# Where SyncE looks at the semaphores of the last eight loads: in front of the last store or behind it

## The chip, the cores and the metric

The kernel runs on one core of a Trainium2 chip. The metric is the device time of one execution in microseconds (us); medians are over runs. The span in a profile goes from the first to the last recorded instruction.

## The reference

It computes the skewness of each of 1024 rows of 8192 float32 numbers:

```python
mean = np.mean(x, axis=-1, keepdims=True)
std = np.std(x, axis=-1, keepdims=True)
z = (x - mean) / (std + 1e-8)
return np.mean(z ** 3, axis=-1).astype(np.float32)
```

## The kernel before

The rows are taken as eight blocks of 128. Each block arrives in two to seven loads, all issued by SyncE into a pool of eight buffers. ScalarE squares and sums, VectorE multiplies and sums the cubes, TensorE sums the columns. A short closing stage makes `skew`, and SyncE stores it (4 KB). The parts that matter here:

```python
for b, widths in enumerate(UNITS):
    ...
    for k, w in enumerate(widths):
        xt = xpool.tile([P, w], FP, tag="x", name=f"x_{b}_{k}")
        nc.sync.dma_start(out=xt, in_=xv[b, :, c0 : c0 + w])
        ...
# ... closing arithmetic of the last two blocks
nc.gpsimd.tensor_tensor(out=rr, in0=var2, in1=expo[:, 0 : NB - F], op=ALU.pow)
nc.vector.tensor_reduce(out=num, ...)
nc.vector.tensor_tensor(out=skew[:, F:NB], in0=num, in1=rr, op=ALU.mult)
nc.sync.dma_start(out=ov, in_=skew)
```

Nothing in this text waits for a semaphore: the framework adds the waits. In the trace of this kernel each DMA that SyncE issues signals on one of eight semaphores, called lanes here, in rotation. At the end of the program the framework makes SyncE check that everything is finished, then all five engines meet (from 89.04 us, when SyncE joins, to the end of the span at 89.729). In the built program, SyncE's end is this (each line an instruction with its waits; `lane3` is the store's):

```
semaphore instruction   lane3 (old value)
store                   VectorE's skew
--- last block of the program
semaphore instruction   lane3 (the store), lane2
semaphore instruction   lane4, lane1
semaphore instruction   lane5, lane0
semaphore instruction   lane6, VectorE
semaphore instruction   lane7, TensorE
drain                   ScalarE
drain                   joins the meeting of the five engines
```

Of the kernel before, what the change touches and what calls it, by code (L numbers as in the profile page):

```python
# [8 lines left out]
FP = mybir.dt.float32  # L9
AF = mybir.ActivationFunctionType  # L10
ALU = mybir.AluOpType
X_AXIS = mybir.AxisListType.X


# [17 lines left out]
def _slices(w):  # L32
    n = -(-w // SUB_MAX)
    step = -(-w // n // 128) * 128
    return [(s, min(s + step, w)) for s in range(0, w, step)]
# [3 lines left out]
def kernel(  # L39
# [5 lines left out]
    nc = tc.nc  # L45
# [13 lines left out]
    xv = x.rearrange("(p b) c -> b p c", b=NB)  # L59
# [11 lines left out]
    def small(name, n):  # L71
        return onep.tile([P, n], FP, tag=name, name=name)
# [22 lines left out]
    def close_first_blocks():  # L95

        m2, m3 = small("m2a", F), small("m3a", F)
        for dst, src in ((m2, s2u), (m3, s3u)):
            nc.vector.tensor_reduce(  # L99
                out=dst, in_=src[:, 0 : F * K].rearrange("p (b c) -> p b c", c=K),  # L100
                axis=X_AXIS, op=ALU.add,
            )
        m1sq, m1sq3, nm1 = small("m1sqa", F), small("m1sq3a", F), small("nm1a", F)
        nc.scalar.copy(out=m1a[:, nw:F], in_=s1ps[:, nw:F])
        nc.scalar.activation(out=m1sq, in_=m1a, func=AF.Square)
        nc.scalar.activation(out=m1sq3, in_=m1a, func=AF.Square, scale=third)
        nc.scalar.activation(out=nm1, in_=m1a, func=AF.Copy, scale=-3.0)
        g = nc.gpsimd
        var, rr = small("vara", F), small("rra", F)
        g.tensor_tensor(out=var, in0=m2, in1=m1sq, op=ALU.subtract)  # L110
        g.tensor_tensor(out=m1sq3, in0=m1sq3, in1=var, op=ALU.add)  # L111
        g.tensor_tensor(out=m1sq3, in0=m1sq3, in1=nm1, op=ALU.mult)  # L112
        g.tensor_tensor(out=m3, in0=m3, in1=m1sq3, op=ALU.add)  # L113
        g.tensor_tensor(out=rr, in0=var, in1=expo, op=ALU.pow)  # L114
        g.tensor_tensor(out=skew[:, 0:F], in0=m3, in1=rr, op=ALU.mult)  # L115

    def close_on_act(b):

        m2, m1sq, nm1, v3 = (small(f"{t}_{b}", 1) for t in ("m2", "m1sq", "nm1", "v3"))
        p1 = s1ps[:, b : b + 1]  # L120
        var = var2[:, b - F : b - F + 1]
        act = nc.scalar.activation
        yield act(out=junk, in_=s2u[:, b * K : b * K + K], func=AF.Copy, accum_out=m2)
        yield act(out=m1sq, in_=p1, func=AF.Square)  # L124
        yield act(out=var, in_=m1sq, func=AF.Identity, scale=-1.0, bias=m2)  # L125
        yield act(out=nm1, in_=p1, func=AF.Copy, scale=-3.0)  # L126
        yield act(out=v3, in_=m1sq, func=AF.Identity, scale=1.0 / 3.0, bias=var)  # L127
        yield act(  # L128
            out=s3u[:, b * K + K - 1 : b * K + K], in_=v3, func=AF.Identity, scale=nm1
        )  # L130

    pending = iter(())
    for b, widths in enumerate(UNITS):
        tp = psum.tile([P, P], FP, tag="tp", name=f"tp_{b}")
        c0 = 0
        j = b * K
        for k, w in enumerate(widths):
            last_unit = b == L and k == len(widths) - 1
            xt = xpool.tile([P, w], FP, tag="x", name=f"x_{b}_{k}")
            nc.sync.dma_start(out=xt, in_=xv[b, :, c0 : c0 + w])  # L140
            c0 += w
            for s, e in _slices(w):
                if last_unit:
                    sq = psum1.tile([P, e - s], FP, tag="sqps", name=f"sqps_{s}")
                else:
                    sq = sqpool.tile([P, e - s], FP, tag="sq", name=f"sq_{b}_{k}_{s}")
                nc.scalar.activation(  # L147
                    out=sq, in_=xt[:, s:e], func=AF.Square, scale=s_scale,
                    accum_out=s2u[:, j : j + 1],
                )  # L150
                cube = sqpool.tile([P, e - s], FP, tag="sq", name="cube") if last_unit else sq
                nc.vector.scalar_tensor_tensor(  # L152
                    out=cube, in0=sq, scalar=1.0, in1=xt[:, s:e],
                    op0=ALU.mult, op1=ALU.mult, accum_out=s3u[:, j : j + 1],
                )
                j += 1
            w_act = S1_ACT.get((b, k), 0)
            if w_act:
                nc.scalar.activation(  # L159
                    out=same[:, 0:w_act], in_=xt[:, w - w_act : w], func=AF.Copy,  # L160
                    scale=inv_n, accum_out=s1a[:, b : b + 1],
                )
            n = (w - w_act) // P
            for c in range(n):
                nc.tensor.matmul(  # L165
                    out=tp, lhsT=xt[:, c * P : (c + 1) * P], rhs=ident,
                    start=(k == 0 and c == 0), stop=(c0 == C and c == n - 1),
                    is_transpose=True,
                )
            if k > 0:  # L170
                next(pending, None)
                next(pending, None)
        tsb = Tsb[b % 2]
        nc.scalar.copy(out=tsb, in_=tp)  # L174
        nc.tensor.matmul(out=s1ps[:, b : b + 1], lhsT=tsb, rhs=onesn, start=True, stop=True)  # L175
        if b == F - 2:
            nc.vector.tensor_tensor(
                out=m1a[:, 0:nw], in0=s1ps[:, 0:nw], in1=s1a, op=ALU.add
            )
        if b == F - 1:  # L180
            close_first_blocks()
        if b >= F:
            pending = close_on_act(b)
    for _ in pending:
# [4 lines left out]
    nc.vector.tensor_reduce(  # L189
        out=num, in_=s3u[:, F * K :].rearrange("p (b c) -> p b c", c=K), axis=X_AXIS, op=ALU.add  # L190
    )
    nc.vector.tensor_tensor(out=skew[:, F:NB], in0=num, in1=rr, op=ALU.mult)  # L192
    nc.sync.dma_start(out=ov, in_=skew)


# [28 lines left out]
```

## Time and profile before

| | us |
|---|---|
| median of three runs (range) | 91.64 (91.61 to 91.72) |
| span of the profiled run, which took 91.50 | 89.73 |
| last load landed | 83.56 |
| `skew` finished on VectorE | 87.20 |
| store started; landed | 87.23; 88.65 |
| SyncE's first drain of the closing line; joins the meeting | 88.98; 89.04 |

The starts to the nanosecond, here and below, are read from the trace's records, since the page rounds to 0.1 us. A semaphore instruction is not counted as work, so the chain of work ends at `skew`; what comes after it has to be read from the instructions of the program's closing line (L219 here).

How to read the views: SPq, DVEq and so on are the engines' instruction queues (SP is SyncE, DVE VectorE, ACT ScalarE, POOL GpSimd, PE TensorE). EVENT_SEMAPHORE is a semaphore instruction; to look at a semaphore is to execute one that waits for it. DRAIN is an instruction of the closing line; SyncE's first one comes after its last look. "Landed" is the time of the last semaphore event recorded for a transfer (the store of the kernel before has 16 of them, from 88.473 to 88.648 us). Views are cut to the lines that are read.

### The profile page before, as it was taken

The numbers are of one execution on the slowest core, as the hardware profiler recorded it, in microseconds if no ns is written. First come the engines' busy times: TensorE is split into PE (matmuls) and PEld (weight loads), VectorE is DVE, ScalarE is ACT, GpSimd is POOL, SyncE is SP. The second block draws the span as 40 slices with busy tenths as digits, with TensorE's granted clock in tenths as the row PEclk, the third lists the DMA queues.
The fourth block names the chain that finished last, engine by engine and source line by source line (L and its number), as shares of the span: only waits on it lengthen the run. The fifth ranks groups of instructions, "written<-read, shape, count | busy, mean of one in ns | idle before, by whom it ended". The sixth has DMA issues, their size and how long they took to land.

```text
span 89.7 us, 1368 instructions
## 1 busy us (share of the span) xinstructions
PE 64.9 (72%) x504; PEld 59.3 (66%) x504; DVE 72.7 (81%) x80; ACT 72.1 (80%) x106; POOL 11.3 (13%) x14
## 2 busy tenths in 40 slices
PE   0003999892882919989998988888987798969710
PEld 0003999791872909979897977877876787848500
DVE  1000498989999298995999999999999999999970
ACT  6003999699991999859898989978979898999950
POOL 3000000000000000000000000000005999900030
PEclk9999999999999997599999999999999999999998
DMA  3999999999999999999999999999999999994000
GB/s 117 351 424 438 424 431 431 431 431 424 446 416 431 424 438 424 424 438 427 415 409 418 419 427 419 421 415 419 409 414 417 404 413 411 421 412 161 0 0 2
DMA packets 4038, 33.64 MB, mean 375 GB/s; under 512 B 576, under 2 KB 576, under 8 KB 2240
## 3 DMA queue, kind: packets, MB, share of 16 engines
q1 hardware_dynamic: 4032, 33.56, 89.7%
q8 instruction: 4, 0.07, 0.3%
q14 instruction: 2, 0.02, 0.0%
HBM read 33.55 MB, written 0.00 MB: 374 GB/s over the span
## 4 chain that ended last, share of the span: by engine, by line
DMA 73%; ACT 13%; issue 5%; DVE 4%; SPq 1%; PE 1%; DVEq 0%; ACTq 0%
DMA x<-in_x_dram 73%; ACT sq L147 9%; DVE sq L152 3%; ACT sqps L147 1%; ACT same L159 1%; SPq L140 1%; PE s1ps L175 1%; ACT tsb L174 0%; ACT s3u L128 0%; ACT v L127 0%; ACT var L125 0%; DVE num L189 0%; ACT m1sq L124 0%; DVE skew L192 0%; ACT nm L126 0%
## 5 line engine op out<-in xcount | busy, mean ns | idle before, releaser
L152 DVE SCALAR_TENSOR_TENSOR sq<-sq,x 128x2048 f32<-128x2048 f32 (+9 forms) x35 | 70.7, 2071 | 13.4 <-ACT sq L147 13.3
L165 PE MATMUL tp<-ident,x 128*128 128x128 f32 x488 | 62.6, 288 | 17.3 <-DMA x<-in_x_dram 17.2
L165 PEld LDWEIGHTS tp<-ident,x 128*128 128x128 f32 x488 | 57.9, 150 | 20.9 <-DMA x<-in_x_dram 12.7
L147 ACT ACTIVATE sq<-x 128x2048 f32<-128x2048 f32 (+9 forms) x35 | 60.6, 1734 | 10.7 <-DMA x<-in_x_dram 9.9
L110 POOL TENSOR_TENSOR vara<-m2a,m1sqa 128x6 f32<-128x6 f32 x1 | 1.8, 1822 | 67.1 <-DVE m3a L99 67.1
L147 ACT ACTIVATION_READ_ACCUMULATOR sq<-x 128x1 f32 x35 | 6.5, 186 | 0.0
L175 PEld LDWEIGHTS s1ps<-onesn,tsb 128*128 128x128 f32 x16 | 2.4, 188 | 5.2 <-ACT tsb L174 5.2
L175 PE MATMUL s1ps<-onesn,tsb 128*128 128x1 f32 x16 | 3.1, 260 | 3.3 <-ACT tsb L174 3.3
L174 ACT COPY tsb<-tp 128x128 f32<-128x128 f32 x8 | 2.0, 256 | 2.0 <-PE tp L165 2.0
L114 POOL TENSOR_TENSOR rra<-vara,expo 128x6 f32<-128x6 f32 x1 | 3.3, 3267 | 0.0
L159 ACT ACTIVATE same<-x 128x1024 f32<-128x1024 f32 x3 | 3.1, 1041 | 0.0
L152 DVE DVE_READ_ACCUMULATOR sq<-sq,x 128x1 f32 x35 | 2.9, 83 | 0.0
L111 POOL TENSOR_TENSOR m1sq3a<-m1sq3a,vara 128x6 f32<-128x6 f32 x1 | 1.9, 1868 | 0.1
L77 ACT ACT_TABLE_LOAD x1 | 1.3, 1283 | 0.7 <-PEq L208 0.7
L187 POOL TENSOR_TENSOR rr<-var,expo 128x2 f32<-128x2 f32 x1 | 0.7, 702 | 7.7 <-ACT var L125 7.7
L152 DVE SCALAR_TENSOR_TENSOR cube<-sqps,x 128x1152 f32<-128x1152 f32 x1 | 1.4, 1350 | 0.0
L113 POOL TENSOR_TENSOR m3a<-m3a,m1sq3a 128x6 f32<-128x6 f32 x1 | 1.2, 1201 | 0.1
L147 ACT ACTIVATE sqps<-x 128x1152 f32<-128x1152 f32 x1 | 1.1, 1136 | 0.1
L115 POOL TENSOR_TENSOR skew<-m3a,rra 128x6 f32<-128x6 f32 x1 | 1.1, 1069 | 0.1
L124 ACT ACTIVATE m1sq<-s1ps 128x1 f32<-128x1 f32 x2 | 0.3, 171 | 0.5 <-PE s1ps L175 0.5
L75 DVE MEMSET onesn<- 128x1 f32 x1 | 0.1, 59 | 0.8 <-PEq L208 0.8
L112 POOL TENSOR_TENSOR m1sq3a<-m1sq3a,nm1a 128x6 f32<-128x6 f32 x1 | 0.7, 697 | 0.0
(28 smaller groups left out, 6.8 us busy)
## 6 DMA issues: line engine op xcount, KB each, us to landing
x<-in_x_dram SPq DMA_DIRECT2D x8, 2048.0 KB, 23.4
x<-in_x_dram SPq DMA_DIRECT2D x4, 1152.0 KB, 27.9
x<-in_x_dram SPq DMA_DIRECT2D x4, 576.0 KB, 8.6
x<-in_x_dram SPq DMA_DIRECT2D x1, 1792.0 KB, 33.0
x<-in_x_dram SPq DMA_DIRECT2D x2, 832.0 KB, 13.9
x<-in_x_dram SPq DMA_DIRECT2D x1, 1024.0 KB, 21.1
x<-in_x_dram SPq DMA_DIRECT2D x2, 512.0 KB, 10.0
x<-in_x_dram SPq DMA_DIRECT2D x1, 960.0 KB, 13.2
```

What stands on the lines that cost most here:

```text
L77: nc.scalar.activation(out=tiny, in_=onesn, func=AF.Square)
L110: g.tensor_tensor(out=var, in0=m2, in1=m1sq, op=ALU.subtract)
L111: g.tensor_tensor(out=m1sq3, in0=m1sq3, in1=var, op=ALU.add)
L113: g.tensor_tensor(out=m3, in0=m3, in1=m1sq3, op=ALU.add)
L114: g.tensor_tensor(out=rr, in0=var, in1=expo, op=ALU.pow)
L115: g.tensor_tensor(out=skew[:, 0:F], in0=m3, in1=rr, op=ALU.mult)
L147: nc.scalar.activation(out=sq, in_=xt[:, s:e], func=AF.Square, scale=s_scale, accum_out=s2u[:, j : j + 1],)
L152: nc.vector.scalar_tensor_tensor(out=cube, in0=sq, scalar=1.0, in1=xt[:, s:e], op0=ALU.mult, op1=ALU.mult, accum_out=s3u[:, j : j + 1],)
L159: nc.scalar.activation(out=same[:, 0:w_act], in_=xt[:, w - w_act : w], func=AF.Copy, scale=inv_n, accum_out=s1a[:, b : b + 1],)
L165: nc.tensor.matmul(out=tp, lhsT=xt[:, c * P : (c + 1) * P], rhs=ident, start=(k == 0 and c == 0), stop=(c0 == C and c == n - 1), is_transp ...
L174: nc.scalar.copy(out=tsb, in_=tp)
L175: nc.tensor.matmul(out=s1ps[:, b : b + 1], lhsT=tsb, rhs=onesn, start=True, stop=True)
```

## The change

Its intent is to let SyncE see, while it would be idle anyway, that the eight last loads have landed, in front of the store, so that the closing check has less left to see once the store has landed.

```diff
+SYNC_DEP = mybir.DependencyInfo(
+    mybir.DependencyClass.Sync, mybir.DependencyReason.DATA
+)
...
+    loads = []
...
-            nc.sync.dma_start(out=xt, in_=xv[b, :, c0 : c0 + w])
+            loads.append(nc.sync.dma_start(out=xt, in_=xv[b, :, c0 : c0 + w]))
...
+    seen = nc.sync.nop()
+    for ld in loads[-8:]:
+        tc.add_manual_dep(seen.ins, ld.ins.name, SYNC_DEP)
     nc.sync.dma_start(out=ov, in_=skew)
```

`seen` is an instruction of SyncE that does nothing; each `SYNC_DEP` makes it wait for one load's semaphore.

## The prediction

> **What bounds the kernel now.** I read the page's chain of work that ended last first, then the last 4 us in order of time, then SyncE's own waits, then the instructions of the program's last line, because the change touches nothing but SyncE at the very end. The chain (section 4 of the page):
>
> ```profile
> DMA 73%; ACT 13%; issue 5%; DVE 4%; SPq 1%; PE 1%; DVEq 0%; ACTq 0%
> ```
>
> The input stream carries 73% of the 89.7 us span: the kernel is bound by 33.55 MB of loads. The change does not alter a load, a buffer or an engine's order, so those first 83.6 us should stay as they are. The chain in order of time, from the last load on:
>
> ```profile
> 76.06 7.50 DMA x<-in_x_dram
> 83.56 0.02 issue
> 83.58 1.26 ACT sqps L147 x2
> ...
> 86.76 0.18 DVE num L189
> 86.95 0.03 issue
> 86.97 0.02 DVEq L192
> 86.99 0.04 issue
> 87.04 0.16 DVE skew L192
> ```
>
> Columns are start, length and what. The last load has landed at 76.06 + 7.50 = 83.56 us; from there 3.64 us of closing arithmetic end at 87.20 with VectorE's skew. The chain stops there, as it follows only working instructions; 89.7 - 87.2 = 2.5 us of the span come after it. SyncE's own waits say what it does around there:
>
> ```profile
> SPq L193 <- DVE skew L192: 10.8, 1, 10.8
> SPq L219 <- DMA out_dram<-skew: 1.1, 1, 1.1
> ```
>
> SyncE is idle for 10.8 us in front of the store, waiting for skew, and after it waits 1.1 us for the store to land. The store and its landing:
>
> ```profile
> L193 SPq DMA_DIRECT2D out_dram<-skew x1: 348/348/348, 87.2 to 87.2; - x1
> ...
> DMA to landing us min/median/max: 1.4/1.4/1.4
> ```
>
> In the last-4-us view the store starts at 87.23, so it has landed at about 88.65. What is left, about 1.08 us, is the program's closing line, L219. Its instructions up to 89.03 us and, in a second view, from 89.03 on:
>
> ```profile
> L219 SPq EVENT_SEMAPHORE  x5: 28/28/28, 88.7 to 88.9; - x5
> ...
> L219 SPq DRAIN  x1: 7/7/7, 89.0 to 89.0; - x1
> ```
>
> ```profile
> L219 POOLq EVENT_SEMAPHORE  x4: 17/17/17, 89.1 to 89.6; - x4
> L219 SPq DRAIN  x2: 7/7/7, 89.0 to 89.3; - x2
> ```
>
> SyncE executes five semaphore instructions one after another, then a drain, then the drain by which it joins the meeting of all five engines. The rounding hides the spacing, so I took it from the trace's records. The store's last landing event is at 88.648; the five semaphore instructions start at 88.665, 88.729, 88.791, 88.855 and 88.917, the drain at 88.982, the joining drain at 89.040, and the meeting ends the span at 89.729. The pitch is (88.982 - 88.665) / 5 = 63.4 ns although each is only 28 ns long by its row. The other engines' first drains start at 85.2 (TensorE), 86.1 (GpSimd), 86.4 (ScalarE) and 87.1 (VectorE): all are waiting for SyncE, which therefore sets the end.
>
> [...] 28 ns reported, 63 ns apart, so pitch and not duration is the cost. [...] The trace has a 0.35 us issue and a 4 KB store that takes 1.42 us from its start to landing[...]; nothing in the change shortens it.
>
> **The change part by part.** The added no-operation vanishes in the build: the order of instructions lists no new one, and its eight waits are shown on the store beside the wait for skew. In the built program an instruction holds at most two waits in front of the one that carries work, so the waits become semaphore instructions:
>
> - In front of the store: before, one semaphore instruction (the store's own lane, an old value) and the store's wait for skew. After, five (one with one wait, four with two) and the same wait. Four more.
> - Behind the store: before, five holding ten waits: the eight load and store lanes, VectorE and TensorE. After, two: first one for VectorE alone, then one for the store's lane with TensorE. The seven lanes without the store need no second look, as SyncE has seen them. Three fewer, and SyncE has one more instruction in all (66 against 65).
>
> Cost in front of the store: the added four take 4 x 63 = 0.25 us. The slowest of them waits for the last load, which lands at 83.56; with one more behind it SyncE stands at the store by about 83.75. Skew is ready at 87.20. So 3.45 us of slack hide it: cost on the path 0.
>
> Gain behind the store: the first remaining instruction waits for VectorE only, which is already done, so it executes in the 1.1 us while the store flies. After the landing there is one semaphore instruction instead of five. The drain starts at 88.665 + 0.063 = 88.728 instead of 88.982: 4 x 63.4 = 0.254 us saved. Everything from the drain on, 89.729 - 88.982 = 0.747 us, should shift unchanged.
>
> Sum: span 89.73 - 0.25 = 89.48 us. The median of the time is 91.64, of which 1.9 us lie outside the span and stay. 91.64 - 0.25 = 91.39 us, a gain of 0.28%.
>
> **Rivals.**
>
> 1. *The semaphores in front delay the store.* Four at 63 ns would cost 0.25 us if they ran after skew, cancelling the gain: 91.64. For it: they do stand in front of the store in SyncE's order. Against it: all eight of their conditions are met at 83.56, 3.6 us before skew[...].
> 2. *The tail's looks are hidden already, or another engine becomes the last.* If the meeting waited for something besides SyncE, the saving would be cut; 91.5 to 91.64. Against it: the next latest drain (VectorE's) starts at 87.1 and is 174 ns long, 1.7 us before SyncE joins at 89.04, far more than 0.25.
> 3. *Only part is saved.* The VectorE look may not be finished when the store lands, if SyncE is slow to cross from the store to the last block (the store's issue ends at 87.58, the first look is ready no later than 88.665). One 63 ns instruction would return: 91.45.
> 4. *The stream shifts.* [...] the stream, which sets 73%, could move by more than the gain. The three times before span 0.11 us (91.61 to 91.72), so I allow about twice that, either way.
>
> **Range and chances.** The mechanism gives 91.39; rivals 3 and 4 lie mostly above it. I put the range at 91.18 to 91.60: the saving of 0.25 with 0.2 us of scatter either way. Two per cent would be 1.83 us in either direction; the whole stretch from skew to the end is 2.5 us, of which 1.42 is the store's own flight, so no removal of semaphore looks can reach it, and a loss of that size would take a stall of which the trace shows no sign. Faster by over 2%: 0.01. Within 2%: 0.98. Slower: 0.01.
>
> **What would show each step right or wrong.** In the changed kernel's profile the closing line should have two SyncE semaphore instructions before its first drain, the first starting before the store lands and the second within some 20 ns of the landing; the drain some 65 ns after that one and the end 0.75 us after the drain. From skew's end to the span's end should be 2.28 us instead of 2.53. The semaphore instructions on the store's line should be five, the last at about 83.7 us, and the store should still start some 30 ns after skew. The prediction is wrong if the store starts later than that after skew, if the landing takes clearly other than 1.42 us, if the first look in the last block comes after the landing, or if the span up to skew moves by more than 0.2 us.

The 0.254 us is four times the 63.4 ns read from the trace.

## The result

The changed kernel took 91.38 us in the median (91.33 to 91.61, six runs) beside 91.62 of the kernel before (91.52 to 91.72, six runs). Ratios, this kernel's time over that of before, are formed from runs taken in the same rounds, so they are not quite the ratio of the medians, nor of the means of all runs: here 0.9978, with a 95% interval of 0.9965 to 0.9991. The gain of 0.24 us between the medians is 0.26%: the same within 2%.

The profiled run of the changed kernel was its slowest, 91.61 us with a span of 89.78, so its span is no shorter than that of before. The views therefore have to be read stretch by stretch. Its chain in order of time (start, length, what):

```profile
76.52 7.35 DMA x<-in_x_dram
83.87 0.02 issue
83.89 1.26 ACT sqps L151 x2
...
87.34 0.16 DVE skew L196
```

The last load landed at 83.87 us, 0.30 later than in the profile of before. From there to the end of `skew` it is 3.64 us in both. So the stream was late in this execution and the closing arithmetic was the same. SyncE's own waits (what waited for what: total, times, longest):

```profile
SPq L198 <- DMA x<-in_x_dram: 6.9, 3, 4.5
SPq L201 <- DVE skew L196: 3.6, 1, 3.6
SPq L227 <- DMA out_dram<-skew: 1.0, 1, 1.0
```

The idle time in front of the store, one wait of 10.8 us before, is now split: 6.9 us on loads and then still 3.6 us on `skew`. The looks come before that 3.6 us, which is slack left over. The looks themselves and the store, in two views of lines L198 and L201 (count, shortest/median/longest in ns, first and last start):

```profile
L198 SPq EVENT_SEMAPHORE  x4: 17/28/2771, 76.9 to 81.1; - x4
```

```profile
L201 SPq EVENT_SEMAPHORE  x1: 28/28/28, 83.9 to 83.9; - x1
L201 SPq DMA_DIRECT2D out_dram<-skew x1: 348/348/348, 87.5 to 87.5; - x1
```

All five semaphore instructions in front of the store start by 83.92 us, and the store starts 28 ns after `skew`, as before (29 ns). The closing line, from 87 us to its first drain:

```profile
L227 SPq EVENT_SEMAPHORE  x2: 17/22/28, 87.9 to 89.0; - x2
...
L227 SPq DRAIN  x1: 7/7/7, 89.0 to 89.0; - x1
```

Two are left instead of five. The first, at 87.93, ran while the store was in flight; only the second, at 88.97, comes after the landing at 88.951. From landing to drain it is 0.084 us, where the kernel before took 0.334. From the end of `skew` to the end of the span it is 2.274 us against 2.530: 0.256 us less.

### The profile page after: what moved, and what is told of

Same layout as the page of the kernel before. It is cut to its first block, busy times and chain, and to the rows that moved or that the text cites. A ratio compares the mean times of both kernels' runs of the same rounds, so it can differ in the third digit from the quotient of the medians.

```text
span 89.8 us, 1369 instructions
## 1 busy us (share of the span) xinstructions
PE 63.8 (71%) x504; PEld 58.0 (65%) x504; DVE 72.7 (81%) x80; ACT 72.0 (80%) x106; POOL 11.3 (13%) x14
## 4 chain that ended last, share of the span: by engine, by line
DMA 57%; DVE 21%; PE 6%; ACT 5%; issue 4%; SPq 3%; DVEq 0%
DMA x<-in_x_dram 57%; DVE sq L156 20%; PE tp L169 6%; SPq L144 3%; ACT sq L151 2%; ACT sqps L151 1%; PE s1ps L179 0%; ACT v L130 0%; ACT s3u L131 0%; ACT tsb L178 0%; ACT var L128 0%; DVE num L193 0%; ACT m1sq L127 0%; DVE skew L196 0%; ACT nm L129 0%
## 5 line engine op out<-in xcount | busy, mean ns | idle before, releaser
L169 PE MATMUL tp<-ident,x 128*128 128x128 f32 x488 | 61.4, 284 | 18.6 <-DMA x<-in_x_dram 18.4
L169 PEld LDWEIGHTS tp<-ident,x 128*128 128x128 f32 x488 | 56.4, 147 | 22.5 <-DMA x<-in_x_dram 14.0
```

What stands on the lines that cost most here:

```text
L169: nc.tensor.matmul(out=tp, lhsT=xt[:, c * P : (c + 1) * P], rhs=ident, start=(k == 0 and c == 0), stop=(c0 == C and c == n - 1), is_transp ...
```

## The experiments

Theory: each semaphore instruction that SyncE executes after the store has landed costs about 63 ns; one executed while SyncE would wait anyway costs nothing. Rivals: the gain on the clock is only scatter; or the looks have to be in front of the store. Each diff is against the changed kernel; `...` marks what is left out, and the comments are added here. `AFTER_IT` is a dependency that sets the order without a wait. All kernels gave correct results. e0_after, e1_behind, e3_half and e4_full ran on one chip with nine runs of the kernel before (median 91.57 us); e2_late, b0_before, e5_after and e6_full on another with nine others (median 91.57).

### The changed kernel again (e0_after, e5_after)

No edit.

> The changed kernel once more, beside the others on one chip. Theory (each semaphore instruction that SyncE executes after the store has landed costs one pitch of 63 ns; those executed earlier cost nothing): 0.25 us under the kernel before, one semaphore instruction between landing and drain, landing to end 0.78 us. Rival (the 0.24 us seen is scatter of the load stream): a ratio to before of 0.999 to 1.001 this time.

> The changed kernel a third time, for the mean. Theory: ratio to before about 0.997, skew's end to the span's end 2.28 us. Rival (no gain on the clock): ratio 0.999 or more as in the second set of runs.

The first of these sets gave 91.53 us (91.31 to 91.60) and a ratio of 0.9990 (0.9976 to 1.0003), an interval that holds both "no gain" and most of the gain; the second gave 91.33 us (91.27 to 91.40) and 0.9971 (0.9957 to 0.9985). On the clock alone, the first set would have supported the rival. The profiles do not: from `skew`'s end to the span's end both have 2.28 us, and from landing to drain 0.084. The "landing to end 0.78" that I had written is an error of addition. It should be the 1.08 us of before less 0.25, 0.83, and 0.829 was measured. The same slip of about 0.05 us is in the expectations of e1_behind (0.78) and e4_full (0.72).

### The look behind the store (e1_behind)

```diff
...
+    st = nc.sync.dma_start(out=ov, in_=skew)
     seen = nc.sync.nop()
+    tc.add_manual_dep(seen.ins, st.ins.name, AFTER_IT)   # order only, no wait
     for ld in loads[-8:]:
         tc.add_manual_dep(seen.ins, ld.ins.name, SYNC_DEP)
-    nc.sync.dma_start(out=ov, in_=skew)
```

> The same look at the eight loads stands behind the store instead of in front of it. Theory (only being ahead of the landing matters, not being ahead of the store): SyncE executes five waits of the eight lanes in the about 1.1 us of the store's flight, 5 x 63 = 0.32 us, so they are done before the landing; the time equals the changed kernel's within 0.05 us, 0.25 us under before; landing to end 0.78 us. Rival (the looks have to be in front of the store): the time is that of the kernel before, landing to end 1.08 us.

It took 91.45 us (91.30 to 91.48), ratio 0.9979 (0.9967 to 0.9992). The four looks (L202) and then the closing line's SyncE instructions up to 89 us:

```profile
L202 SPq EVENT_SEMAPHORE  x4: 17/28/28, 87.8 to 88.0; - x4
```

```profile
L231 SPq EVENT_SEMAPHORE  x2: 17/22/28, 88.3 to 88.9; - x2
L231 SPq COMPARE_BRANCH  x1: 33/33/33, 88.1 to 88.1; - x1
L231 SPq DRAIN  x1: 7/7/7, 89.0 to 89.0; - x1
```

The looks ran from 87.85 on, behind the store's issue, and were finished by 88.3. The branch to the closing line (COMPARE_BRANCH) carries the wait for one lane, and the first semaphore instruction behind it is the look for VectorE. The store landed at 88.871. From landing to drain it is 0.082 us, from `skew` to the end 2.276, the changed kernel's numbers. So being in front of the store is not what mattered in this kernel. Being ahead of its landing was.

### Half of the loads (e3_half)

```diff
-    for ld in loads[-8:]:
+    for ld in loads[-4:]:
```

> The look covers the last four loads only. In the built program three semaphore instructions stand in front of the last drain instead of five (before) or two of which one is early (changed). The first of the three waits for the store's lane, so all three come after the landing. Theory: 2 x 63 = 0.13 us saved against before, half of the whole change; landing to end 0.95 us. Rival (the gain comes from one particular wait or from scatter): the whole 0.25 us or nothing.

The ratio was 0.9997 (0.9985 to 1.0010), at 91.60 us (91.40 to 91.70), with the median above that of before: the clock shows nothing of the 0.13 us. For the profiled run, the slowest of the five at 91.70, the profile gives a reason: its last load landed at 83.859, late in the range found below. For the other four no landing is on record, so the missing gain is not explained for them. The tail is where the theory puts it, between the two kernels:

```profile
L227 SPq EVENT_SEMAPHORE  x3: 28/28/1047, 87.9 to 89.1; - x3
L227 SPq DRAIN  x1: 7/7/7, 89.1 to 89.1; - x1
```

Three semaphore instructions stand before the drain, and from landing to drain it is 0.191 us, against 0.084 with one and 0.334 with five. The longest is recorded with 1047 ns. I had expected it to wait for the store first. In the built program its first condition is a load, met at once, so it had started at 87.92 and was waiting for its second, the store. That made it 18 ns cheaper than two more pitches (0.084 + 2 x 0.063 = 0.209).

### No semaphore instruction behind the landing (e4_full, e6_full)

```diff
...
+    st = nc.sync.dma_start(out=ov, in_=skew)
     seen = nc.sync.nop()
-    for ld in loads[-8:]:
-        tc.add_manual_dep(seen.ins, ld.ins.name, SYNC_DEP)
-    nc.sync.dma_start(out=ov, in_=skew)
+    tc.add_manual_dep(seen.ins, st.ins.name, AFTER_IT)
+    for i in loads[-8:] + [mm, la, pw, last]:   # last of PE, ACT, POOL, DVE
+        tc.add_manual_dep(seen.ins, i.ins.name, SYNC_DEP)
```

> The look stands behind the store and covers the eight loads and the last instructions of TensorE, ScalarE, GpSimd and VectorE, so that the drain itself waits for the store's lane and no semaphore instruction is left between landing and drain. Theory: one more pitch of 63 ns saved than the changed kernel, 5 x 63 = 0.32 us under before; landing to end 0.72 us. Rival (the first instruction after a landing has a floor, or SyncE is not done with six waits before the landing): no better than the changed kernel.

> The kernel with no semaphore instruction between landing and drain once more, for the mean. Theory: skew's end to the span's end 2.21 us, 0.32 us under before, ratio to before about 0.9965. Rival: no better than the changed kernel of the same set.

The two sets gave 91.40 us (91.20 to 91.44), ratio 0.9973 (0.9960 to 0.9985), and 91.26 us (91.19 to 91.33), ratio 0.9965 (0.9952 to 0.9977). Here is the closing line of the first of them, SyncE alone, up to the first drain:

```profile
L231 SPq COMPARE_BRANCH  x1: 33/33/33, 88.1 to 88.1; - x1
L231 SPq DRAIN  x1: 7/7/7, 88.8 to 88.8; - x1
```

No semaphore instruction is left; the drain waits for the store itself and starts 17 ns after its landing, in both profiles. From `skew` to the end it is 2.207 and 2.209 us, 0.07 less than the changed kernel and 0.32 less than before. Against the kernel before, both intervals exclude 1. Against the changed kernel its median is lower in both sets (91.40 against 91.53, 91.26 against 91.33), but the single runs overlap, so that step rests on the profile's 0.07 us.

### The looks held back until skew is ready (e2_late)

```diff
...
-    seen = nc.sync.nop()
-    for ld in loads[-8:]:
-        tc.add_manual_dep(seen.ins, ld.ins.name, SYNC_DEP)
+    prev = None
+    for part in (loads[-4:], [last], loads[-8:-4]):   # last: VectorE's skew
+        seen = nc.sync.nop()
+        for i in part:
+            tc.add_manual_dep(seen.ins, i.ins.name, SYNC_DEP)
+        if prev is not None:
+            tc.add_manual_dep(seen.ins, prev.ins.name, AFTER_IT)
+        prev = seen
```

In the built program the wait for `skew` then stands in the first of the five semaphore instructions.

> The look stands in front of the store as in the changed kernel, but its first wait is for skew, so that all five semaphore instructions in front of the store come after skew. Theory (a look costs a pitch only when SyncE is what the end waits for): the store starts about 5 x 63 = 0.3 us later after skew than its 0.03 us in the other kernels; behind the landing one semaphore instruction as in the changed kernel; skew's end to the span's end 2.28 + 0.3 = 2.58 us, so 0.05 us over the kernel before and 0.3 us over the changed one. Rival (looks in front of the store are free because SyncE reads satisfied semaphores at no cost): 2.28 us as in the changed kernel.

It took 91.64 us (91.53 to 91.74), ratio 1.0006 (0.9993 to 1.0018): the gain is gone. In order of time around the store:

```profile
87.14 0.16 DVE L199 TENSOR_TENSOR skew<-num,rr 128x2 f32<-128x2 f32 x1
87.63 0.35 SPq L209 DMA_DIRECT2D out_dram<-skew  x1
```

The store starts 0.323 us after `skew` ends (0.028 in the changed kernel), so the five semaphore instructions cost 0.295 us once SyncE is what the end waits for. From landing to drain it is 0.084, as in the changed kernel. From `skew` to the end 2.564 was measured, 2.58 expected. So here the satisfied semaphores were not read for free (0.295 us for five instructions, 59 ns each); in the changed kernel the reading is hidden.

### The kernel before against itself (b0_before)

No edit to the kernel before.

> The kernel before against itself, as a control. Theory (the load stream's end wanders by some 0.3 us between executions whatever the kernel, while the tail is fixed): the last load lands anywhere from 83.5 to 83.9 us in the profile, skew's end to the span's end 2.53 us within 0.02 us, and a ratio of 0.999 to 1.001. Rival (only the changed kernel's stream wanders): the last load at 83.56 within 0.05 us.

Its ratio was 1.0002 (0.9990 to 1.0015), 91.65 us (91.47 to 91.75). The last load landed at 83.775, 0.21 later than in the first profile of the same kernel, and its tail was unchanged at 2.529 us. So the stream wanders without the change. The ten profiles side by side (us):

| kernel | semaphore instructions between landing and drain | last load landed | landing to drain | `skew`'s end to span's end |
|---|---|---|---|---|
| before; again | 5; 5 | 83.563; 83.775 | 0.334; 0.333 | 2.530; 2.529 |
| half of the loads | 3 (the first started before the landing) | 83.859 | 0.191 | 2.384 |
| changed; again; again | 1; 1; 1 | 83.867; 83.620; 83.671 | 0.084; 0.084; 0.084 | 2.274; 2.277; 2.278 |
| look behind the store | 1 | 83.783 | 0.082 | 2.276 |
| looks held back | 1 | 83.662 | 0.084 | 2.564 |
| none left; again | 0; 0 | 83.679; 83.565 | 0.017; 0.017 | 2.207; 2.209 |

One rival these variants can't tell apart: that the cost goes with the waits and not with the instructions, since each of the counted instructions holds two waits. The ten traces can. Where nothing had to be waited for, SyncE's next instruction started 60 to 70 ns after a semaphore instruction with two waits (64 cases) and 48 to 64 ns after one with a single wait (31 cases). So a second wait in the same instruction adds little, and most of the cost is the instruction's.

## Why the prediction was right

**Size.** Predicted 91.39 us, measured 91.38 in the median. The hundredth is partly luck, as executions of one kernel are up to 0.3 us apart. What was right beyond luck is the mechanism: the stretch from `skew` to the end was to fall from 2.53 to 2.28 us and fell to 2.274 to 2.278 in three profiles.

**Front of the store.** The step "cost on the path 0" holds: the last look starts 57 ns after the last load, the store 28 ns after `skew`. The held-back looks show what hides it, since there the same instructions cost 0.295 us. In the kernel before, the looks of the closing line that had nothing to wait for followed each other at 62 to 64 ns. Rival 1 was a real mechanism without its occasion here.

**Behind the store.** "One semaphore instruction instead of five" holds, and so does the pitch: (0.334 - 0.084) / 4 = 0.0625 us, and 0.067 for the last one, which the version without any removes. The look for VectorE ran at 87.93, 1.0 us before the landing, so rival 3 did not occur. Everything from drain to end stayed at 0.744 to 0.752 us, so rival 2 did not either. The store's landing took 1.410 to 1.422 us in all ten profiles, so it was carried over as assumed.

**The stream.** Rival 4 is the one that happened. My own test said that the prediction would be wrong if the span up to `skew` moved by more than 0.2 us, and in the profiled run it moved by 0.31. That test was badly chosen: I took the scatter from three runs that span 0.11 us, while the two profiles of the kernel before alone are 0.21 us apart at the last load, and the ten profiles 0.30. The stream is as late in runs of either kernel, so the shift is not shown to come from the change. On the clock, the mean gain over all runs was 0.20, 0.13 and 0.24 us in the three sets (91.617 - 91.417, 91.604 - 91.470, 91.578 - 91.336). That is 0.19 on average, somewhat under the 0.25 of the tail. With such scatter it stays open whether the difference means anything. What makes the stream late in one execution was not studied. The prediction's "the input stream carries 73% of the span" is also less firm than it reads: the second profile of the same kernel has 52% DMA and 23% VectorE in its chain. The tail is not touched by that.

**A small slip.** I put 1.9 us outside the span by setting the median of three runs against the span of another. For the profiled run itself it is 91.50 - 89.73 = 1.77; in the ten profiled runs it was 1.77 to 1.87, which adds to the scatter on the clock. As the prediction carried this part over unchanged, the slip did not touch the predicted gain.

## What to carry to other kernels

After the last store of this kernel had landed, every instruction left on the engine that closes the program was on the path, at about 63 ns for each semaphore instruction. In another kernel, check in the profile that this engine is the last to join the closing meeting. Look at what it still has to check, and have it checked earlier: in front of the store, if that is long before the data is ready, or while the store is in flight. Put between the last result and its store, the same look cost its full pitch here. When a change is smaller than the scatter of the load stream, measure the stretch it touches in the profile, from a fixed event to the end, and let the clock only confirm the sign.

## What the traces show of semaphore instructions

- Recorded start and length. Not every semaphore instruction of SyncE with two waits is recorded with 28 ns: 16 on the loads' line (L140) of the kernel before are recorded as 1.3 to 5.1 us long, one as 1047 ns in the version with half of the loads, one as 2771 ns in the changed kernel. The latter starts at 81.119, 17 ns after the first of its two loads landed (81.102), and ends at 83.890, 23 ns after the second (83.867). So this record starts 17 ns after the condition listed first was met, and the waiting for the second appears as its length. "Listed first" is not "met first": in the kernel before, the first instruction of the closing line lists the store ahead of a load that had landed at 83.563, and it starts at 88.665, 17 ns after the store's landing.
- One wait or two. From a semaphore instruction with one wait to the next instruction the ten traces have 48 to 64 ns (31 cases), with two 60 to 70 ns (64 cases), where nothing had to be waited for. These instructions are recorded with 17 and 28 ns.
- A branch that carries a wait. In the version with the look behind the store, the closing branch held one, was recorded at 88.094 for 33 ns, and the next instruction started 158 ns after that start (seen once). In the changed kernel no branch is recorded there, and the next instruction started 45 ns after the store's issue had ended.
